# Splitting weights for float32r matmuls: the low parts through accumulating DMAs

## The chip, the cores and the metric

The kernel runs on one core of one Trainium2 chip. The time is what the device takes for one execution, in microseconds (us), from launch to end. A profiled execution has a span of its own, from its first to its last instruction. The core has five engines that run their own instruction streams in order: PE (TensorE, matrix products), DVE (VectorE), ACT (ScalarE), POOL (GpSimd) and SP (SyncE, which here only issues DMAs). They meet through semaphores. Sixteen DMA engines move data between HBM and SBUF, the on-chip memory of 128 partitions.

## The reference

One layer of a streaming encoder, for 512 frames of width 1024, all in float32:

```python
xn = rmsnorm(h, norm_mix_g)
u = xn @ w_in                                   # 7 x 1024 columns
q, k, v, xr, gr, ga, gb = split(u)
ya = chunked_band_attention(q, k, v, rel_table) @ w_attn_out
hr = rg_lru(causal_depthwise_conv(xr, conv_w, conv_b), ...)
yb = (hr * gelu(gr)) @ w_rnn_out
g_a, g_b = sigmoid([ga, gb] + b_merge)
h = h + (g_a * ya + g_b * yb) @ w_o
hn = rmsnorm(h, norm_ffn_g)
g, up = split(hn @ w_ffn_in)                    # 2 x 2816 columns
h = h + (silu(g) * up) @ w_ffn_out
out = rmsnorm(h, final_norm_g)
```

## The kernel before

PE multiplies in float32r, which keeps fewer bits than float32. To get float32 accuracy, each operand is held as two float32r parts: the high part is the rounded number, the low part is what the rounding left. A product `s @ m` is made of three matmuls (`mm3`): high with high (L70), and the two mixed ones (L71, L72). The low part of a weight is read by one of the mixed two: by the third (L72) where the weights are the stationary operand, by the second (L71) where they are the moving one (v, wo, fo).

The weights come in **chunks**, planned in the order of their use: xr, gr, ga, gb (the projections for the recurrent branch and the gates, in pairs of 128-column blocks, j = 0, 2, 4, 6), qk and v (attention), yb, ya, wo, fg and fu (into the feed-forward part), fo (out of it). A plain chunk is one or two times, for wo four times, a tile of 512 KB: 128 partitions by 1024 numbers. The chunks fg2 to fu20 go another way (a Strassen-like scheme, with sums of blocks) and are made by `weight_sums`; the change does not touch them.

For each tile `prefetch` does three things:

- `load` issues a DMA from HBM on SP's queue into a buffer with the tag `raw` (L145). There are three of them, so a load waits until the raw tile three before it has been read for the last time. The Strassen chunks' loads use the same three and one more. Other loads stand in the same SP queue: in attention `bias_tile` (L393) fetches the bias of each head into one of two buffers.
- ACT writes the high part into `hl[:, 0]` of a buffer with the tag `whl` (L76). There are four in `wp`; wo1 and half of the fo chunks have four more of their own. A chunk that feeds 48 matmuls takes two buffers.
- DVE writes the low part, raw minus high, into `hl[:, 1]` (L77). Both lines are in the helper `split`, which also splits activations. Only the second tile of the very first chunk (xr0) has its low part made by POOL (L206).

`weights(name)` makes sure that the named chunk and the one after it have been written down in the program before PE's matmuls on the named one (with other distances in a few places: two for xr, three for fo, none in the first steps). So while PE works on one chunk, ACT and DVE make the next. A `whl` buffer comes free when PE has used it for the last time; the buffers of a chunk are used by its first 128 columns and again by its second.

In order, the stages are: norm and transposes of x; xr, gr, ga, gb with the recurrence between them (40 to 181 us of the span); yb together with the first scores (to 250 us); attention over 16 heads, with the remaining qk, v and ga projections laid between the heads as filling work (to some 420 us); ya; wo; fg0 and fu0; the Strassen chunks (to 756 us); fo and the final norm. In attention POOL also divides the exponentials by their sums (L627), makes one copy of k's low part (L583) and masks the bias (L394); in the recurrence it makes low parts of activations (L457, L500) and one elementwise step (L486).

The order on each engine is laid down when the program is built, from the program order and an estimated timeline; on the chip each engine takes its instructions in that order and waits where it must.

Of the kernel before, what the change touches and what calls it, by code (L numbers as in the profile page):

```python
# [10 lines left out]
AF = mybir.ActivationFunctionType  # L11
ALU = mybir.AluOpType
# [24 lines left out]
def block_kernel(ctx: ExitStack, tc: tile.TileContext, x, norm_mix_g, w_in, b_merge, rel_table,  # L37
# [3 lines left out]
    pe, dve, act, pool, sp = nc.tensor, nc.vector, nc.scalar, nc.gpsimd, nc.sync  # L41
# [20 lines left out]
    def f(ap):  # L62
        return ap.bitcast(F32)
# [10 lines left out]
    def split(hi, lo, src):  # L74

        act.activation(hi, src, AF.Copy)  # L76
        dve.tensor_sub(lo, src, f(hi))  # L77
# [55 lines left out]
    def load(name, k):  # L133
        _, parts, rows, kts = chunks[index[name]]
        wide = sum(width for *_, width in parts)
        n = min(4 * CW // wide, kts - k)
        at = rows + k * P
        pl, bufs = wp, 3
        if name in strassen and name[0] == "f":
            loads[0] += 1  # L140
            pl, bufs = (room[0], 1) if loads[0] % 4 == 0 else (wp, 3)
        raw = pl.tile([P, n, wide], F32, tag="raw", bufs=bufs, name=f"raw_{name}_{k}")
        to = 0
        for src, col, width in parts:
            sp.dma_start(out=raw[:, :, to:to + width],  # L145
                         in_=src[at:at + n * P, col:col + width].rearrange("(k p) e -> p k e", p=P))
            to += width
        raws[name, k] = raw
# [5 lines left out]
    def weight_sums(name):  # L154

        for k in (0, 4):
            if (name, k) not in raws:
                load(name, k)
        r0, r1 = raws.pop((name, 0)), raws.pop((name, 4))
        a11, a21, a12, a22 = r0[:, :, 0:P], r0[:, :, P:CW], r1[:, :, 0:P], r1[:, :, P:CW]  # L160
        sc = room[0]
        s21, s34 = (sc.tile([P, 2, 4, P], F32, tag=tag, bufs=1, name=f"{tag}_{name}")
                    for tag in ("s21", "s34"))
        s2, s1, s3, s4 = s21[:, 0], s21[:, 1], s34[:, 0], s34[:, 1]
        dve.tensor_add(s1, a21, a22)
        dve.tensor_sub(s2, s1, a11)
        other = pool if name in ("fg2", "fu2", "fg4") else dve
        other.tensor_sub(s3, a11, a21)
        other.tensor_sub(s4, a12, s2)
        blocks_ = {}  # L170
        for group in ((("a11", a11), ("a12", a12)), (("s2", s2), ("s1", s1)), (("s3", s3), ("s4", s4)), (("a22", a22),)):
            pl, tag, bufs = sc, "a22", 2
            if len(group) == 2:
                slots[0] += 1
                pl, tag, bufs = (sc, "whl", 1) if slots[0] % 5 == 0 else (wp, "whl", 4)
            o = pl.tile([P, len(group), 2, 4, P], F32R, tag=tag, bufs=bufs, name=f"whl_{name}_{group[0][0]}")
            together = group[0][0] in ("s2", "s3") and name != "fg2"
            if together:
                split(o[:, :, 0], o[:, :, 1], (s21 if group[0][0] == "s2" else s34)[:])
            for i, (key, src) in enumerate(group):  # L180
                if not together:
                    split(o[:, i, 0], o[:, i, 1], src)
                blocks_[key] = o[:, i]
        return blocks_

    def prefetch(n):
        while len(made) < min(n, len(chunks), index.get(barrier[0], len(chunks))):
            name, parts, rows, kts = chunks[len(made)]
            if name in strassen:
                made.append(weight_sums(name))  # L190
                continue
            tiles = []
            wide = sum(width for *_, width in parts)
            step = 4 * CW // wide
            for k in range(0, kts, step):
                n_ = min(step, kts - k)
                if name in extra:
                    hl = extra[name].tile([P, 2, n_, wide], F32R, tag="whl", bufs=4, name=f"whl_{name}_{k}")
                else:
                    hl = wp.tile([P, 2, n_, wide], F32R, tag="whl", bufs=4, name=f"whl_{name}_{k}")  # L200
                if (name, k) not in raws:
                    load(name, k)
                raw = raws.pop((name, k))
                if len(made) == 0 and k:
                    act.activation(hl[:, 0], raw[:], AF.Copy)
                    pool.tensor_sub(hl[:, 1], raw[:], f(hl[:, 0]))  # L206
                else:
                    split(hl[:, 0], hl[:, 1], raw[:])
                tiles.append(hl)
            made.append(lambda part, k, at, tiles=tiles, step=step: tiles[k // step][:, part, k % step, at])  # L210

    def weights(name, ahead=1):
        prefetch(index[name] + 1 + ahead)
        return made[index[name]]
# [70 lines left out]
    for name, w in (("r", w_rg_r), ("i", w_rg_i)):  # L285
        raw = nm.tile([P, 8, P], F32, name=f"wrg_raw_{name}")
# [146 lines left out]
    for name, raw in zip("ri", wrg_raw):  # L433
        hl = rw2.tile([P, 2, 8, P], F32R, bufs=1, name=f"wrg_{name}")
# [305 lines left out]

    hsq = []
    prefetch(index["wo1"] + 1)
    for t in range(NT):
        q2 = cp.tile([P, 2], F32, tag="hsq2", bufs=2, name=f"hsq2_{t}")
# [75 lines left out]
    room[0] = sc  # L820
    barrier[0] = "fo0_16"
    prefetch(index["fg2"] + 1)

    for i, name in enumerate(("fg0", "fg0", "fu0", "fu0")):
# [129 lines left out]
```

## Time and profile before

| | us |
|---|---|
| time, median of 2 runs | 901.03 (900.98 to 901.07) |
| time of the profiled execution | 900.88 |
| its span, first to last instruction | 899.1 |
| mean granted TensorE clock | 0.993 |

The span is 1.8 us shorter than the time of the same execution. Lines of the profile name the engine, the source line (L77 is line 77 of the kernel), the operation, the tile it writes and those it reads (`whl_fo<-raw_fo,whl_fo`; buffer numbers are left out), and partitions x elements. A view that groups instructions gives their count, their durations, the idle time of the engine just before them, and what ended it. A name with a q at its end (SPq) is an engine's queue: the instruction that issues a DMA, not the transfer.

### The profile page before, as it was taken

What the parts mean: (1) busy time and instruction counts of PE and PEld (TensorE: products, weight loads), DVE (VectorE), ACT (ScalarE), POOL (GpSimd) and SP (SyncE); (2) the same over time, 40 slices, a digit from 0 to 9 for tenths busy, and PEclk for the clock granted to TensorE, in tenths of its full rate; (3) what the DMA queues carried; (4) which work ended last, traced back from release to release, by engine and by line L of the source; (5) the groups of instructions that cost most, each with busy time, mean ns of one, the idle gap of its engine ahead of it and who ended that gap; (6) DMA issues with size and microseconds to landing.
All of it is one profiled execution on the core that took longest, in us unless ns stands there. A gap on an engine that the chain in (4) does not pass through costs nothing.

```text
span 899.1 us, 13343 instructions
## 1 busy us (share of the span) xinstructions
PE 881.4 (98%) x5220; PEld 778.1 (87%) x5220; DVE 553.6 (62%) x863; ACT 473.5 (53%) x841; POOL 133.1 (15%) x168
## 2 busy tenths in 40 slices
PE   8999999999999999999999999899999999999997
PEld 5988888888888889797888889899999999888886
DVE  5776556553466676666546455998888887453203
ACT  7566546642257666666533365556555556623103
POOL 4012112120023222222100002510000001300100
PEclk9999999999999999999999999899999999999999
DMA  8323222423332232331123620333433333353002
GB/s 261 95 71 117 85 84 90 118 94 94 105 104 73 74 111 64 93 95 60 66 63 124 217 66 30 117 117 95 140 96 94 96 118 108 98 184 120 30 1 94
DMA packets 85023, 89.05 MB, mean 99 GB/s; under 512 B 5344, under 2 KB 73552, under 8 KB 84960
## 3 DMA queue, kind: packets, MB, share of 16 engines
q1 hardware_dynamic: 83584, 84.73, 30.7%
q10 hardware_dynamic: 1376, 3.47, 1.1%
q8 instruction: 41, 0.67, 0.3%
q14 instruction: 22, 0.18, 0.1%
HBM read 86.05 MB, written 2.14 MB: 98 GB/s over the span
## 4 chain that ended last, share of the span: by engine, by line
PE 92%; DVE 3%; ACT 2%; issue 1%; DMA 1%; POOL 1%; SPq 0%; DVEq 0%; ACTq 0%; POOLq 0%
PE po_out L70 5%; PE po_out L72 5%; PE po_out L71 5%; PE p_fu L71 2%; PE p_fu L70 2%; PE p_fu L72 2%; PE p_fg L72 2%; PE p_fg L71 2%; PE p_fg L70 2%; PE o L659 2%; PE po_ga L70 2%; PE pT L639 2%; PE po_ga L71 2%; PE po_ga L72 2%; PE po_ya L70 2%; PE po_ya L71 2%
## 5 line engine op out<-in xcount | busy, mean ns | idle before, releaser
L70 PE MATMUL po_out<-whl_fo,act_hi 128*128 128x512 f32 (+1 forms) x198 | 73.2, 369 | 0.0
L71 PE MATMUL po_out<-whl_fo,act_hi 128*128 128x512 f32 (+1 forms) x198 | 72.9, 368 | 0.0
L72 PE MATMUL po_out<-whl_fo,act_lo 128*128 128x512 f32 (+1 forms) x198 | 72.1, 368 | 0.0
L77 DVE TENSOR_TENSOR whl_fo<-raw_fo,whl_fo 128x1024 fp32r<-128x1024 f32 x22 | 27.5, 1259 | 47.0 <-ACT whl_fo L76 47.0
L627 POOL TENSOR_SCALAR p<-p,rl 128x128 f32<-128x128 f32 (+1 forms) x64 | 37.4, 605 | 84.4 <-DVE rl L625 83.8
L76 ACT ACTIVATE whl_fo<-raw_fo 128x1024 fp32r<-128x1024 f32 x22 | 23.0, 1056 | 50.6 <-PE po_out L72 36.1
L624 ACT ACTIVATE p<-p,m 128x128 f32<-128x128 f32 (+3 forms) x64 | 35.5, 555 | 22.0 <-DVE m L623 21.6
L623 DVE CUSTOM_DVE_ANT_0 p<-s,bias 128x128 f32<-128x128 f32 (+3 forms) x64 | 29.8, 487 | 22.6 <-PE s L621 21.8
L72 PEld LDWEIGHTS po_out<-whl_fo,act_lo 128*128 128x128 f32 x198 | 37.2, 188 | 6.9
L70 PEld LDWEIGHTS po_out<-whl_fo,act_hi 128*128 128x128 f32 x198 | 37.2, 188 | 6.6
L71 PEld LDWEIGHTS po_out<-whl_fo,act_hi 128*128 128x128 f32 x198 | 37.2, 188 | 6.6
L659 PE MATMUL o<-pp,v 128*128 128x256 f32 (+2 forms) x128 | 35.4, 337 | 3.0 <-ACT pp L76 3.0
L839 POOL TENSOR_TENSOR act_lo<-act,act_hi 128x1024 fp32r<-128x1024 f32 x4 | 10.5, 2624 | 184.1 <-ACT act_hi L838 182.7
L71 PE MATMUL po_v<-whl_v,xnT 128*128 128x256 f32 x128 | 36.9, 288 | 0.0
L77 DVE TENSOR_TENSOR pp<-pT,pp 128x256 fp32r<-128x256 f32 (+2 forms) x64 | 30.4, 486 | 10.4 <-ACT pp L76 10.0
L70 PE MATMUL po_v<-whl_v,xnT 128*128 128x256 f32 x128 | 36.5, 285 | 0.0
L72 PE MATMUL po_v<-whl_v,xnT 128*128 128x256 f32 x128 | 36.4, 284 | 0.0
L76 ACT ACTIVATE pp<-pT 128x256 fp32r<-128x256 f32 (+2 forms) x64 | 26.5, 433 | 10.8 <-DVE pp L77 6.3
L77 DVE TENSOR_TENSOR whl_fu_s<-s_fu,whl_fu_s 128x1024 fp32r<-128x1024 f32 x20 | 25.3, 1280 | 5.7 <-ACT whl_fu_s L76 5.6
L71 PE MATMUL po_xr<-xnT,whl_xr 128*128 128x512 f32 (+1 forms) x80 | 27.9, 354 | 0.6 <-DVE xnT L327 0.5
L639 PE MATMUL pT<-ident,p 128*128 128x128 f32 x160 | 27.5, 273 | 0.7 <-POOL p L627 0.7
L70 PE MATMUL po_gr<-xnT,whl_gr 128*128 128x512 f32 (+1 forms) x80 | 27.8, 349 | 0.1
(354 smaller groups left out, 3089.9 us busy)
## 6 DMA issues: line engine op xcount, KB each, us to landing
raw_fg<-in_w_ffn_in_dram SPq DMA_DIRECT2D x22, 512.0 KB, 4.5
raw_fu<-in_w_ffn_in_dram SPq DMA_DIRECT2D x22, 512.0 KB, 3.6
raw_fo<-in_w_ffn_out_dram SPq DMA_DIRECT2D x22, 512.0 KB, 4.3
raw_qk<-in_w_in_dram SPq DMA_DIRECT2D x32, 256.0 KB, 3.3
raw_xr<-in_w_in_dram SPq DMA_DIRECT2D x8, 512.0 KB, 5.0
raw_gr<-in_w_in_dram SPq DMA_DIRECT2D x8, 512.0 KB, 3.5
raw_ga<-in_w_in_dram SPq DMA_DIRECT2D x8, 512.0 KB, 3.6
raw_gb<-in_w_in_dram SPq DMA_DIRECT2D x8, 512.0 KB, 3.7
```

The costliest lines, as they stand in the source:

```text
L70: pe.matmul(o, sh, mh, start=start, stop=False, skip_group_check=parts)
L71: pe.matmul(o, sh, ml, start=False, stop=False, skip_group_check=parts)
L72: pe.matmul(o, sl, mh, start=False, stop=stop, skip_group_check=parts)
L76: act.activation(hi, src, AF.Copy)
L77: dve.tensor_sub(lo, src, f(hi))
L623: dve.tensor_tensor_reduce(prob[qb][:], sc[:, 0:w], bias[:, S - w:S], -1.0, 3e38, ALU.add, ALU.min, nmax[:, qb:qb + 1])
L624: act.activation(prob[qb][:], prob[qb][:], AF.Exp, bias=nmax[:, qb:qb + 1], scale=-1.0, accum_out=lsum[:, qb:qb + 1])
L627: pool.tensor_scalar(prob[qb][:], prob[qb][:], rl[:, qb:qb + 1], 1.0, ALU.mult, ALU.mult)
L639: pe.transpose(pt[:, at * P:(at + 1) * P], prob[qb][:, kb * P:(kb + 1) * P], ident[:])
L659: pe.matmul(po[:, S - n:S], st, pp[i][:, part, lo:lo + n], start=kb == 0 and part == 0, stop=kb == NT - 1 and part == 1)
L839: (pool if i in (0, 1, 2, 4) else dve).tensor_sub(lo[:], o[:], f(hi[:]))
```

## The change

Every plain chunk but xr0, gr0, fg0 and fu0 gets its low parts in another way. ACT makes the high part as before. POOL writes minus raw into the place of the low part; since that place is float32r, what arrives is minus the rounded number, that is minus the high part. Then POOL issues a DMA that adds raw, read from SBUF, to what stands there. DVE has no part in it any more. The first four plain chunks are split as before, and so are all activations.

```diff
                 if len(made) == 0 and k:
                     act.activation(hl[:, 0], raw[:], AF.Copy)
                     pool.tensor_sub(hl[:, 1], raw[:], f(hl[:, 0]))
+                elif name not in ("xr0", "gr0", "fg0", "fu0"):
+
+                    act.activation(hl[:, 0], raw[:], AF.Copy)
+                    pool.tensor_scalar(hl[:, 1], raw[:], -1.0, None, ALU.mult)
+                    pool.dma_start(out=hl[:, 1], in_=raw[:], accum_op=ALU.add)
                 else:
                     split(hl[:, 0], hl[:, 1], raw[:])
                 tiles.append(hl)
```

## The prediction, made before the changed kernel had run

> **What bounds the kernel.** I read the busy times first, then stretches of the span, then what PE waited for. The first line gives each engine's busy time, its share of the span and its instructions.
>
> ```profile
> PE 881.4 (98%) x5220; PEld 778.1 (87%) x5220; DVE 553.6 (62%) x863; ACT 473.5 (53%) x841; POOL 133.1 (15%) x168
> ```
>
> PE is busy for all but 17.7 us of the span of 899.1. The next view cuts the span by stage; its columns after the stretch are its length, busy time (instructions) of PE, weight loads, DVE, ACT and POOL, the granted clock, the DMA share and GB/s.
>
> ```profile
> core 0: us, PE busy (x) PEld busy (x) DVE busy (x) ACT busy (x) POOL busy (x), PEclk, DMA share, GB/s
> ...
> 40.00:181.00 141.00, 141.00 (x621) 116.23 (x620) 92.72 (x121) 85.97 (x112) 26.52 (x24) 1.00 0.32 97
> ...
> 250.00:420.00 170.00, 165.09 (x972) 145.32 (x971) 110.42 (x249) 110.03 (x249) 46.11 (x91) 0.99 0.30 89
> 420.00:494.00 74.00, 74.00 (x348) 60.96 (x347) 40.84 (x69) 32.27 (x57) 4.74 (x10) 1.00 0.23 74
> ...
> 756.00:828.00 72.00, 72.00 (x371) 61.07 (x370) 34.23 (x32) 31.74 (x38) 8.10 (x3) 1.00 0.39 125
> ```
>
> In the stages with plain chunks PE has no gap at all, but for 4.9 us in attention (170.00 - 165.09). So DVE's 92.72 of 141 us in the first stretch are hidden, and taking work from DVE cannot shorten it. What PE waited for, all in all:
>
> ```profile
> PE o L659 <- ACT pp L76: 3.0, 2, 1.5
> PE q_fg L70 <- ACT whl_fg_s L76: 1.9, 1, 1.9
> ...
> PE pT L639 <- POOL p L627: 0.7, 2, 0.3
> ...
> PE po_gr L72 <- DVE whl_gr L77: 0.3, 1, 0.3
> ```
>
> A low part of a plain weight made PE wait once, for 0.3 us, and that one is gr0's, which the change leaves alone. The 3.0 us for the transposed probabilities are a chain ACT to DVE in attention that a freer DVE may shorten. Hence a gain has a ceiling of about 5 us (the 4.9 of attention), and the question is how much of the cover the slower way to a low part uses up.
>
> **Removed: DVE's subtractions.**
>
> ```profile
> L77 DVE TENSOR_TENSOR whl_fo<-raw_fo,whl_fo x22: 1218/1225/2002, 756.2 to 854.5; 128x1024 fp32r<-128x1024 f32 x22
> ...
> L77 DVE TENSOR_TENSOR whl_qk<-raw_qk,whl_qk x16: 1211/1226/1422, 167.4 to 383.2; 128x1024 fp32r<-128x1024 f32 x16
> ...
> L77 DVE TENSOR_TENSOR whl_gr<-raw_gr,whl_gr x8: 1209/1225/2284, 15.5 to 151.3; 128x1024 fp32r<-128x1024 f32 x8
> ...
> L77 DVE TENSOR_TENSOR whl_xr<-raw_xr,whl_xr x7: 1216/1226/1254, 8.6 to 135.1; 128x1024 fp32r<-128x1024 f32 x7
> ```
>
> 22 for fo, 16 for qk, six each for gr and xr (two and one are of the excluded chunks), and eight each for ga, gb, v, yb, ya and wo by the plan of chunks: 98 tiles. At 1.225 us they are 120 us of DVE. By the windows PE gains from this only in attention; I take 2 us of the 3.0.
>
> **Added: 98 negations and 98 accumulating DMAs.** A negation is one operation on 128x1024. The nearest rows are POOL's own elementwise ones:
>
> ```profile
> L486 POOL TENSOR_SCALAR a<-u 128x512 f32<-128x512 f32 x8 | 4.9, 618 | 33.8 <-DVE u L484 33.7
> ...
> L839 POOL TENSOR_TENSOR act_lo<-act,act_hi 128x1024 fp32r<-128x1024 f32 x4 | 10.5, 2624 | 184.1 <-ACT act_hi L838 182.7 <-DMA g_fin<-in_final_norm_g_dram 1.4
> ```
>
> Below is 0.62 (the same kind on half the elements), above 2.62 (the same size with two inputs); I take twice 0.618, 1.2 us, the same kind. No POOL-issued DMA and no accumulating one stand in this trace. What stands there are SP's loads:
>
> ```profile
> q1 hardware_dynamic: 83584, 84.73, 30.7%
> q10 hardware_dynamic: 1376, 3.47, 1.1%
> ```
> ```profile
> L145 SPq DMA_DIRECT2D raw_wo<-in_w_o_dram x8: 367/368/368, 470.0 to 497.3; - x8
> ...
> DMA to landing us min/median/max: 3.5/3.6/8.0
> ```
>
> Issue: 0.37 us (SP's row) at least, 2.62 (POOL's long row above) at most, if the issue occupies POOL like a long instruction of its own; I take 1.0, between the two and nearer to the row of an issue. Transfer: q1 used 0.307 x 16 x 899.1 = 4416 engine-us for 84.73 MB, so a tile of 0.524 MB takes 27.3, or 1.7 us of all 16 engines; q10, by the same sum, 1.5 us. The add reads two tiles and writes one: one pass, 1.5, is the floor; two passes at q10's price, 3.0, is my value; two at q1's with one load ahead, 2 x 1.7 + 1.7 = 5.1, is the top. A load's landing of 3.5 less its 1.7 leaves 1.8 of latency. So the add lands 4.8 us after its issue (3.3 to 6.9).
>
> The Trainium skill, "Collectives: The Full Stack", section "The bandwidth ceiling: the fold count and why AG ≠ RS ≠ AR", says that the add inside a DMA costs nothing in itself, but its second source halves the rate. No run here shows it yet; by it the transfer would be the same two passes.
>
> From a free buffer with its raw tile there, the low part then takes 1.2 + 1.0 + 4.8 = **7.0 us** (4.3 to 12.1). Before it took ACT's 1.06 and DVE's 1.23, 2.3 us. It is 4.7 us later (2.0 to 9.8). Set against the typical time until PE wants it, here for ga2:
>
> ```profile
> L72 PE MATMUL po_ga<-xnT,whl_ga x16: 389/389/398, 88.8 to 99.0; 128*128 128x512 f32 x16
> L76 ACT ACTIVATE whl_ga<-raw_ga x2: 1061/1062/1062, 72.1 to 74.8; 128x1024 fp32r<-128x1024 f32 x2
> ...
>   PE po_xr L72: 2.6, 2
> ```
>
> ACT starts on each tile when PE's po_xr frees the buffer, at 72.1 and 74.8, and the first L72 on it comes at 88.8, so there are 16.7 us: 7.0 fits, and 12.1 too. PE takes 10.2 us over 15 steps of three matmuls, 10.9 for a chunk; the DMA engines would have two loads and two adds in it, 3.4 + 6.0 = 9.4 us. Full, but not over.
>
> **The tight places.** ga0, at the start:
>
> ```profile
> L72 PE MATMUL po_ga<-xnT,whl_ga x16: 389/389/398, 39.5 to 51.2; 128*128 128x512 f32 x16
> L76 ACT ACTIVATE whl_ga<-raw_ga x2: 1045/1052/1059, 30.2 to 35.3; 128x1024 fp32r<-128x1024 f32 x2
> ```
>
> The first tile has 9.3 us. The second is first read four steps (2.7 us) later, at 42.2, so it has 6.9 against 7.0: with some queueing 0.5 us. For wo:
>
> ```profile
> L76 ACT ACTIVATE whl_wo<-raw_wo x8: 1046/1062/1062, 480.8 to 505.5; 128x1024 fp32r<-128x1024 f32 x8
> L77 DVE TENSOR_TENSOR whl_wo<-raw_wo,whl_wo x8: 1218/1224/1226, 481.9 to 506.6; 128x1024 fp32r<-128x1024 f32 x8
> ```
> ```profile
> L752 DVE SCALAR_TENSOR_TENSOR h<-po_h,h x8: 683/692/692, 503.2 to 540.2; 128x512 f32<-128x512 f32 x8
> ...
> L727 ACTq DMA_DIRECT2D h<-in_x_dram x4: 357/443/459, 494.8 to 496.2; - x4
> ```
>
> Eight tiles pass through three raw buffers. The last load went out at 497.3, when tile 5 had been split, and its low part was done at 507.8 (506.6 + 1.22), in the middle of the eight products that ended between 503.2 and 540.2. Tile 5's add lands 4.7 us later, and so do the last load and its own add: the load came beside the four h loads and took the longest, 8.0 us; later it would come after them and take 3.6, which makes good the first delay, but the add at the end costs 4.7 again. So the last low part is some 4.7 late. If PE's order is as before it waits 4 us; if its order moves the other products of the first half forward, 0; if each reuse adds its delay, 9. I take 4. At fo's start:
>
> ```profile
> L71 PE MATMUL po_out<-whl_fo,act_hi x22: 388/393/399, 766.3 to 784.4; 128*128 128x512 f32 x22
> ...
> L76 ACT ACTIVATE whl_fo<-raw_fo x7: 1038/1050/1062, 755.1 to 780.4; 128x1024 fp32r<-128x1024 f32 x7
> ```
>
> 11.2 us: nothing at 7.0, 1 us at 12.1.
>
> **What is queued behind.** On POOL 98 x 2.2 = 216 us come in (133 becomes 349, 39%). In the window of attention its 46 us get some 24 x 2.2 = 53 more, and the division of the probabilities (L627), for which pT waited 0.7 us, stands in that queue; I set this against what DVE's relief gives beyond the 2 us. On SP a load waits for its raw buffer, now until the add has landed, and what is behind it waits too, above all the bias of a head:
>
> ```profile
> 283.92 0.37 SPq L145 DMA_DIRECT2D raw_v<-in_w_in_dram  x1
> 285.26 7.06 SPq L393 DMA_DIRECT2D bias<-ext_d  x2
> ...
> 333.65 0.37 SPq L145 DMA_DIRECT2D raw_v<-in_w_in_dram  x1
> 334.30 8.08 SPq L393 DMA_DIRECT2D bias<-ext_d  x2
> ```
>
> Here a bias follows within 1.3 and 0.7 us on a load that a low part had released; I count four such heads. Each gets its bias up to 4.7 us later, 19 us in all; the filling matmuls between the heads cover most. I take 4.
>
> Sum: 0.5 + 4 + 4 - 2 = +6.5 us on the profiled execution's 900.9, so 907; the median of the runs, 901.03, is the same within 0.2.
>
> **The rivals.**
> - *The cover holds and attention gains.* PE's order follows the later low parts, nothing stalls, and the 4.9 us come in: 896. For it speaks the 16.7 us; against it that wo's eighth tile came 507.8, late already. 0.10.
> - *SP's queue.* The four heads are not covered, and the delay of 4.7 each goes through to the transposes: 19 instead of 4, 922. It decides from about 4.5 us of lateness per head, since 18 us are the 2%. For it speaks that pT has waited for POOL's p at all, against it PE's mere 4.9 us of gaps in attention. 0.10.
> - *DVE holds POOL up.* The slowest DVE subtractions took 2284 and 2002 ns beside a median of 1225: something excluded them for about 1 us. If each negation and each issue waits out one DVE instruction of 1.2 us, the low part takes 9.4, with a second one behind it 12: ga0 then loses 3 to 5 us, wo 9, fo 1, attention 7: +20, 921. The Trainium skill, "SBUF — State Buffer", section "Who interferes with whom", has such a lock between a DVE instruction with two SBUF inputs and a POOL instruction that reads SBUF, and adds that a DVE in a two-port mode keeps POOL from writing descriptors; by that rule the trace's long subtractions agree, and no run yet shows the descriptors. 0.08.
> - *The DMA engines become the bound.* From (10.9 - 3.4) / 2 = 3.75 us per add on they cannot keep up with PE. At the top, 5.1, a chunk takes 13.6 us, 2.7 more; over 20 dense chunks (12 of xr to gb, 4 of yb, 4 of ya) that is 54 us, 955. Against it: 5.1 needs three tiles' worth of traffic per add. 0.15.
>
> The add might also not give the low part at all, if POOL's rounding differs from ACT's; that would not change the time.
>
> **The numbers.** My forecast has 0.56, between 899 and 918. A measurement of this kernel tells 2%, 18 us, from no change. Faster by more than that has no mechanism, as PE's gaps are 17.7 us in all: 0.01. Slower by more: 0.10 + 0.08 + 0.15 = 0.33. Within: 0.66. The range goes from the gain's 896 up to 938, short of the middle of the last rival, and leaves out some 0.14.
>
> **What would show it.** In the changed profile: no L77 for whl tiles but the excluded and Strassen ones, DVE near 434 us; POOL near 350; a DMA queue of its own with some 51 MB; PE waiting for a DMA that writes whl_wo and whl_ga, not whl_gr or whl_gb; adds landing near 5 us after their issue. If PE waits for whl in every dense chunk, the DMA rival is right; if pT or s waits with bias loads late on SP, the queue; if POOL's negations are far over 1.2 us, the lock. I am wrong on the main point if an add takes more than 9 us from issue to landing, or if DVE's relief shows where PE had no gap.

## The result, and the profile after

The changed kernel takes 991.88 us (median of 2 runs, 990.47 and 993.30) beside 901.03: the ratio is 1.101, with a 95% interval from 1.094 to 1.108. It is 10% slower, where 907 was forecast and 938 was the end of the range. The profiled execution is the one of 990.47 us, with a span of 988.7.

From the page of the changed kernel, the busy time of each engine and two of the DMA queues (packets, MB, share of 16 engines):

```profile
PE 906.8 (92%) x5220; PEld 788.9 (80%) x5220; DVE 445.2 (45%) x765; ACT 473.7 (48%) x841; POOL 479.4 (48%) x364
...
q0 software_dynamic: 14112, 51.39, 29.3%
q1 hardware_dynamic: 83584, 84.73, 27.0%
```

The change did what it says: DVE has 98 instructions less, POOL 196 more, and a new queue moves 51.39 MB. But PE is now idle for 81.9 us (988.7 - 906.8) instead of 17.7, and the same 5220 matmuls keep it busy for 25.4 us more. The 89.6 us that the span grew are these two: 64.2 of gaps and 25.4 of slower matmuls. POOL is at 479 us instead of the 349 that I had summed up.

What PE waited for in the changed kernel (total us, times, longest):

```profile
PE po_out L71 <- DMA whl_fo<-raw_fo: 18.9, 7, 7.0
PE po_h L71 <- DMA whl_wo<-raw_wo: 11.2, 3, 8.3
PE s L625 <- ACT kh L587: 8.4, 2, 5.8
PE q_fg L70 <- ACT whl_fg_s L76: 5.9, 1, 5.9
PE s L625 <- DVE m L628: 5.4, 4, 1.8
```

The low parts of fo and wo, now written by a DMA, come late; and in attention PE waits for ACT and DVE, which have no more to do than before. The lines behind the new work on POOL, from the groups of instructions of the changed kernel, and from the view of the tile whl_fo from 826 us on (durations min/median/max in ns; the last line is the adds' time from issue to landing):

```profile
L210 POOL TENSOR_SCALAR whl_fo<-raw_fo 128x1024 fp32r<-128x1024 f32 x22 | 61.0, 2783 | 52.4 <-DMA raw_fo<-in_w_ffn_out_dram 46.4 <-PE q_fg L72 5.1 <-PE q_fu L72 1.0
...
L211 POOL DMA_DIRECT2D whl_qk<-raw_qk x16 | 14.3, 928 | 0.6 <-issue 0.6
```
```profile
L210 POOL TENSOR_SCALAR whl_fo<-raw_fo x20: 2761/2767/3096, 824.0 to 956.3; 128x1024 fp32r<-128x1024 f32 x20
...
DMA to landing us min/median/max: 4.5/6.7/11.1
```

A negation takes 2.77 us, not 1.2; the issue of an add 0.93, and the add lands after 4.5 us at best. POOL's order in fo, from the timeline of POOL (start, duration, then what and how often; in brackets the idle time before and what ended it):

```profile
864.26 8.25 POOL L210 TENSOR_SCALAR whl_fo<-raw_fo 128x1024 fp32r<-128x1024 f32 x3 [9.78 <-DMA raw_fo<-in_w_ffn_out_dram]
872.46 2.68 POOL L211 DMA_DIRECT2D whl_fo<-raw_fo  x3
885.02 8.25 POOL L210 TENSOR_SCALAR whl_fo<-raw_fo 128x1024 fp32r<-128x1024 f32 x3 [9.88 <-DMA raw_fo<-in_w_ffn_out_dram]
```

POOL negates three tiles, then issues three adds, then waits for the next three raw tiles, which can only be loaded into the buffers that these adds have read. One round is 8.25 + 2.68 + 9.88, or 20.8 us from 864.26 to 885.02. PE's matmuls on three tiles take 16.4 (5.45 us per tile, half of the 10.9 per chunk of the prediction), so each round leaves a gap of some 4.4 us. SP's queue shows the same loop; in the waits of SP before and after, the fo loads are held up by

```profile
SPq L145 <- DVE whl_fo L77: 70.8, 19, 14.8
```
```profile
SPq L145 <- DMA whl_fo<-raw_fo: 128.5, 19, 16.4
```

Where the time went, by stages that I cut at the first matmul on po_h (wo) and on po_out (fo); the last five rows are experiments told below:

| us | start to wo | wo, f0, Strassen | fo | span |
|---|---|---|---|---|
| before | 494.6 | 271.4 | 133.0 | 899.1 |
| after | 522.6 | 304.0 | 162.1 | 988.7 |
| short negation (e1_two_op) | 498.7 | 284.1 | 133.5 | 916.3 |
| long negation, in turn (e5_in_turn) | 537.4 | 283.9 | 136.9 | 958.2 |
| after's order, short (e12) | 498.4 | 301.3 | 134.7 | 934.4 |
| e1's order, long (e13) | 514.8 | 289.0 | 141.4 | 945.2 |
| POOL subtracts, no add (e3) | 498.8 | 273.7 | 133.1 | 905.6 |

Each of the three parts lost about 30 us (28.0, 32.6 and 29.1). But the first cut does not part the same work everywhere. In the changed kernel PE does a single matmul on po_h at 522.6, goes back to 44 matmuls of ya, and takes up wo at 533.2; from the views of the tiles po_ya and whl_wo (count, durations, then first and last start):

```profile
L72 PE MATMUL po_ya<-aT,whl_ya x64: 390/397/400, 485.4 to 533.0; 128*128 128x512 f32 x64
...
L71 PE MATMUL po_h<-whl_wo,mT x64: 387/389/794, 533.2 to 591.8; 128*128 128x512 f32 x64
```

Of the other rows only e12 has the same 44, some 10 us of PE without a gap. Counted to the last matmul of ya instead, the changed kernel lost 39 us up to wo, 22 from there to fo, and 29 in fo.

### The profile page after: what moved, and what is told of

Same layout as the page of the kernel before. It is cut to its first block, busy times and chain, and to the rows that moved or that the text cites. A ratio compares the mean times of both kernels' runs of the same rounds, so it can differ in the third digit from the quotient of the medians.

```text
span 988.7 us, 13608 instructions
## 1 busy us (share of the span) xinstructions
PE 906.8 (92%) x5220; PEld 788.9 (80%) x5220; DVE 445.2 (45%) x765; ACT 473.7 (48%) x841; POOL 479.4 (48%) x364
## 3 DMA queue, kind: packets, MB, share of 16 engines
q0 software_dynamic: 14112, 51.39, 29.3%
## 4 chain that ended last, share of the span: by engine, by line
PE 48%; DMA 27%; POOL 11%; ACT 5%; issue 4%; DVE 4%; SPq 0%; POOLq 0%; ACTq 0%; DVEq 0%
DMA whl_fo<-raw_fo 5%; POOL whl_fo L210 3%; DMA raw_fo<-in_w_ffn_out_dram 3%; DMA raw_wo<-in_w_o_dram 2%; PE p_fg L72 2%; PE p_fg L70 2%; PE p_fg L71 2%; DMA raw_v<-in_w_in_dram 2%; PE p_fu L70 2%; PE p_fu L71 2%; PE p_fu L72 2%; DMA whl_gr<-raw_gr 2%; DMA raw_qk<-in_w_in_dram 2%; DMA whl_wo<-raw_wo 2%; PE o L664 2%
## 5 line engine op out<-in xcount | busy, mean ns | idle before, releaser
L210 POOL TENSOR_SCALAR whl_fo<-raw_fo 128x1024 fp32r<-128x1024 f32 x22 | 61.0, 2783 | 52.4 <-DMA raw_fo<-in_w_ffn_out_dram 46.4
L72 PE MATMUL po_out<-whl_fo,act_lo 128*128 128x512 f32 (+1 forms) x198 | 74.5, 383 | 0.0
L210 POOL TENSOR_SCALAR whl_qk<-raw_qk 128x1024 fp32r<-128x1024 f32 x16 | 44.9, 2810 | 36.5 <-DMA raw_qk<-in_w_in_dram 18.8
L71 PEld LDWEIGHTS po_out<-whl_fo,act_hi 128*128 128x128 f32 x198 | 39.1, 198 | 28.4 <-DMA whl_fo<-raw_fo 21.3
L882 DVE TENSOR_TENSOR h<-po_out,h 128x512 f32<-128x512 f32 (+1 forms) x9 | 5.7, 629 | 110.6 <-PE po_out L72 110.6
L77 DVE TENSOR_TENSOR pp<-pT,pp 128x512 fp32r<-128x512 f32 (+1 forms) x64 | 30.6, 488 | 43.2 <-ACT pp L76 42.8
L70 PEld LDWEIGHTS po_out<-whl_fo,act_hi 128*128 128x128 f32 x198 | 38.5, 195 | 7.2
L76 ACT ACTIVATE pp<-pT 128x512 fp32r<-128x512 f32 (+1 forms) x64 | 26.6, 432 | 32.1 <-PE pT L644 28.2
L70 PE MATMUL po_v<-whl_v,xnT 128*128 128x256 f32 x128 | 37.6, 295 | 3.0 <-ACT whl_v L209 2.6
L71 PE MATMUL po_v<-whl_v,xnT 128*128 128x256 f32 x128 | 38.1, 298 | 2.1 <-DMA whl_v<-raw_v 2.1
L72 PE MATMUL po_v<-whl_v,xnT 128*128 128x256 f32 x128 | 37.5, 293 | 0.0
L210 POOL TENSOR_SCALAR whl_wo<-raw_wo 128x1024 fp32r<-128x1024 f32 x8 | 22.4, 2805 | 31.0 <-DMA raw_wo<-in_w_o_dram 30.9
L71 PE MATMUL po_h<-whl_wo,mT 128*128 128x512 f32 x64 | 25.9, 410 | 11.2 <-DMA whl_wo<-raw_wo 11.2
```

Of the source, the lines that this page charges most:

```text
L70: pe.matmul(o, sh, mh, start=start, stop=False, skip_group_check=parts)
L71: pe.matmul(o, sh, ml, start=False, stop=False, skip_group_check=parts)
L72: pe.matmul(o, sl, mh, start=False, stop=stop, skip_group_check=parts)
L210: pool.tensor_scalar(hl[:, 1], raw[:], -1.0, None, ALU.mult)
```

## The experiments

Each time stands beside runs of the kernel before on the same chip (902.03 for e1 to e4, 900.82 for e5 to e7, 901.55 from e8 on). Where no interval is given it is one execution. Three theories stood at the start. A: the loop through the three raw buffers is too long. B: POOL's queue. C: the DMA engines are too full.

**e1_two_op: the negation in another form.** The row of 618 ns that I had doubled is of an instruction with two operations (L486 multiplies and adds); the change's has one. So the same negation, written with two:

```diff
-                    pool.tensor_scalar(hl[:, 1], raw[:], -1.0, None, ALU.mult)
+                    pool.tensor_scalar(hl[:, 1], raw[:], -1.0, 1.0, ALU.mult, ALU.mult)
```

> The negation is written with two immediates (times -1, times 1), the form of the row that took 618 ns on 512 elements, instead of one operation; the value is the same. Changed kernel: 990.5 us, negation 2.77 us. Theory A (the loop through the three raw buffers, load + negation + issue + add, is as long as PE takes for three tiles, so PE stalls wherever there is no stock): the negation falls to about 1.2 us, the loop from some 16 to 14.4 us, and the stalls of wo, fo and attention shrink: about 955. Theory B (POOL's queue: 3.7 us a tile among its other work): POOL falls from 479 to about 325 us busy, about 925. Theory C (the 16 DMA engines are too full, share 0.75, and loads and adds slow each other): traffic is the same, no less than 980. If the form makes no difference to the negation's 2.77 us, the run tells nothing of the three.

Measured: 918.07. Groups of POOL's instructions in it, and what PE waited for:

```profile
L210 POOL TENSOR_SCALAR whl_qk<-raw_qk 128x1024 fp32r<-128x1024 f32 x16 | 17.9, 1122 | 33.2 <-issue 12.8 <-PE po_k L72 9.7 <-PE po_yb L72 6.1
L211 POOL DMA_DIRECT2D whl_qk<-raw_qk x16 | 14.2, 906 | 4.5 <-POOL whl_qk L210 4.5
```
```profile
PE po_h L71 <- DMA whl_wo<-raw_wo: 5.6, 1, 5.6
PE q_fg L70 <- ACT whl_fg_s L76: 5.0, 1, 5.0
```

The negation takes 1.12 us, and 74 of the 91 us are gone, with the same adds and the same traffic. That refutes C, and it is more than A or B had given it (955 and 925). What is left is at wo, as forecast, and just behind it.

**e2_act_neg: the negation on ACT.**

```diff
-                    pool.tensor_scalar(hl[:, 1], raw[:], -1.0, None, ALU.mult)
+                    act.activation(hl[:, 1], raw[:], AF.Copy, scale=-1.0)
```

> ACT writes minus raw (Copy with scale -1) in place of POOL; POOL only issues the adds. ACT gets 98 x 1.06 = 104 us (474 to 578), POOL loses 98 x 2.8 = 274 (479 to about 205). Theory A: the loop is 1.7 us shorter, and an issue no longer stands behind the next negation: about 950. Theory B: nearly all of the loss on POOL's account goes: about 915. Theory C: no less than 980.

Measured: 922.53. POOL, with the issues alone, is down to 207 us, ACT up to 562. PE waits 5.4 us at wo and in a few places for ACT. It comes out near e1: the negation has to be short, and on which of the two engines it runs made 4 us.

**e3_pool_sub: POOL subtracts, no DMA.**

```diff
-                    pool.tensor_scalar(hl[:, 1], raw[:], -1.0, None, ALU.mult)
-                    pool.dma_start(out=hl[:, 1], in_=raw[:], accum_op=ALU.add)
+                    pool.tensor_sub(hl[:, 1], raw[:], f(hl[:, 0]))
```

> POOL makes the low part in one subtraction (raw minus high) and there is no add by DMA. The low part is then ready 1.06 + about 2.6 = 3.7 us after the buffer is free. Theory A: 905, since the loop is 3.5 + 3.7 = 7 us and raw comes free at POOL's end. Theory B: POOL is still busy for some 390 us in the same places, so much of the loss stays: about 940. Theory C: the adds' traffic is gone, so 905 as well; this run separates B from A and C.

Measured: 907.37. A subtraction takes POOL 2.4 to 2.7 us, about as long as the slow negation, and costs only 5 us in all. So an instruction of 2.7 us per tile on POOL is not enough, and B falls as it stood; it takes the add behind it.

**e4_raw_fo: more raw buffers for half of fo.** Half of the fo chunks get three raw buffers of their own.

```diff
+        if name in extra and name != "wo1":
+            pl, bufs = extra[name], 3
         raw = pl.tile([P, n, wide], F32, tag="raw", bufs=bufs, name=f"raw_{name}_{k}")
```

> Half of the fo chunks (those that have whl buffers of their own) get three raw buffers of their own, so fo's loads have six instead of three; all else as in the changed kernel. Theory A: fo, 162 us long against 133 before, loses most of its 29 us: about 965, and its PE waits for whl_fo go from 18.9 to under 5 us. Theory B: the loads come sooner but POOL is as busy: 985. Theory C: no change in fo, 990.

Measured: 981.02, a gain of some 10 us, all in fo (162 to 152), and less than A expected. POOL's timeline in it shows why:

```profile
847.86 14.30 POOL L212 TENSOR_SCALAR whl_fo<-raw_fo 128x1024 fp32r<-128x1024 f32 x5 [5.02 <-DMA raw_fo<-in_w_ffn_out_dram]
862.11 1.76 POOL L213 DMA_DIRECT2D whl_fo<-raw_fo  x2
```

With six buffers the order has five negations in a row, 14.3 us, ahead of the first add, and PE waited 12.4 us for a low part once. So the order of POOL's queue may be what costs: the adds stand behind the negations of tiles that are needed later.

**e5_in_turn: negation, add, negation, add.** The long negation stays, each queued behind the add of the tile before.

```diff
+                    with tc.issue_after(lastadd[0]) if lastadd[0] is not None else ExitStack():
-                    pool.tensor_scalar(hl[:, 1], raw[:], -1.0, None, ALU.mult)
-                    pool.dma_start(out=hl[:, 1], in_=raw[:], accum_op=ALU.add)
+                        pool.tensor_scalar(hl[:, 1], raw[:], -1.0, None, ALU.mult)
+                    lastadd[0] = pool.dma_start(out=hl[:, 1], in_=raw[:], accum_op=ALU.add).ins
```

> Edit: the slow one-operation negation (2.77 us) stays, but each negation is queued on POOL behind the add of the tile before, so that POOL's order is negation, add, negation, add. Nothing is left out. Theory D (the length of the negation is what costs): POOL's time per tile is 2.77 + 0.9 either way, the waits for whl_fo and whl_wo stay, and it takes 975 to 995. Theory E (the order costs: the changed kernel lets three negations go ahead of three adds, so that the first add is issued 5.5 us late and all three land behind each other at 4.7, 6.7 and 10 us): in turn a raw buffer is held for 3.6 + 2.8 + 0.9 + 4.7 = 12 us, or 4.0 per tile with three buffers, under PE's 5.45; fo falls from 162 to about 134, attention from 283 to about 255, and only wo still waits, some 4 to 8 us more than with the short negation (918): 920 to 932.

Measured: 959.98, between D and E. fo fell to 136.9, as E expects, and the part from wo to the Strassen stage got 20 us shorter, of which 10 are the matmuls of ya that are back in front of the cut. Attention, from the first matmul on po_yb to the first on po_ya, stayed at 278.8 us (283.3 in the changed kernel, 251.0 before), which E does not explain, and the start of wo came 15 us later, 10 of them those matmuls.

**e6_short_wo_dve: short negation, wo left to DVE.**

```diff
-                elif name not in ("xr0", "gr0", "fg0", "fu0"):
+                elif name not in ("xr0", "gr0", "fg0", "fu0") and name[:2] != "wo":
```

> Edit: the negation in the form with two operations (1.05 to 1.27 us), and wo's eight tiles keep DVE's subtraction; nothing is left out. With the short negation everywhere the time was 918.1 beside 902.0, with 53.2 us in wo (45.4 before), 26.2 in f0 (24.6) and 204.7 in the Strassen stage (201.4). Theory F (the 7.8 of wo come from its last tiles' adds, and f0 and the Strassen stage are late because the raw buffers of wo come free late): without wo's adds all three return, and it takes 903 to 907, though 90 adds with their 47 MB still run. Theory C (the traffic of the adds itself slows the loads or PE): 910 or more.

Measured: 905.78, ratio 1.0057 (1.0036 to 1.0078). F holds: wo is back at 45.4, f0 at 24.6, the Strassen stage at 200.9. Ninety adds, with short negations, cost 5 us in all; wo's eight had cost some 11 (918.07 - 902.03, less 5).

**e7_attention_only: the gain that I had hoped for.** The add, with the short negation, only for 20 tiles of attention:

```diff
-                elif name not in ("xr0", "gr0", "fg0", "fu0"):
+                elif name[:2] == "qk" and name != "qk0" or name[0] == "v" and name != "v0":
```

> Edit: the add only for the chunks of attention after the first (qk1 to qk7, v1 to v3), 20 tiles, with the negation of two operations; all the rest is as before; nothing is left out. Theory G (as I forecast: a DVE with 24 us less to do in attention lets PE gain there, up to the 4.9 us of its gaps): 897 to 901 beside 901 to 902. Theory H (DVE does not set attention's pace: with all of the short adds attention took 252.4 beside 251.0, so there is nothing to gain): 901 to 904.

Measured: 901.12 beside 900.82, ratio 1.0005 (0.9994 to 1.0016). H: no gain from a freer DVE, in the place with the best chance of one. Attention itself took 249.5 us instead of 251.0 in the one execution profiled, which the times do not show.

**e8_pool_high and e9_in_turn_pool_high: who stands in ACT's queue.** In attention, the timeline of the changed kernel shows PE's longest gap like this:

```profile
274.95 0.90 POOL L211 DMA_DIRECT2D whl_qk<-raw_qk  x1
...
279.61 0.37 SPq L145 DMA_DIRECT2D raw_v<-in_w_in_dram  x1
...
285.29 1.06 ACT L209 ACTIVATE whl_v<-raw_v 128x1024 fp32r<-128x1024 f32 x1 [4.86 <-DMA raw_v<-in_w_in_dram]
...
286.37 0.59 ACT L665 ACTIVATE oacc<-o 64x512 f32<-64x512 f32 x1
286.99 0.59 ACT L587 ACTIVATE kh<-po_k 64x512 fp32r<-64x512 f32 x1
...
287.63 1.12 PE L625 MATMUL s<-kh,q 128*128 128x256 f32 x3 [5.77 <-ACT kh L587]
```

The tile of v is loaded late, because its buffer was held until the add that was issued at 274.95 had landed: SP waited 9.7 us for that `DMA whl_qk<-raw_qk` before it issued the load at 279.61, and the load took 5.7 us to land. ACT, in order, waits for it with the high part, behind which stands the key part that PE needs. Such waits for raw tiles in attention are not in the trace of before. The edit lets POOL make the high parts of attention's 40 tiles, in e9 on top of e5_in_turn:

```diff
-                    act.activation(hl[:, 0], raw[:], AF.Copy)
+                    if name in ("ga4", "ga6") or name[:2] in ("qk", "yb") and name != "qk0" or name[0] == "v" and name != "v0":
+                        pool.tensor_copy(hl[:, 0], raw[:])
+                    else:
+                        act.activation(hl[:, 0], raw[:], AF.Copy)
```

> Edit: the changed kernel, but for the 40 tiles that are split during attention (qk1 to qk7, v1 to v3, yb, ga4, ga6) the high part is copied by POOL, right before the negation, and not by ACT. Nothing is left out. In the changed kernel ACT's high part waited at the head of ACT's queue for a raw tile that was loaded late (whl_v for 4.86 us at 285.29, with oacc, kh and pp behind it, and PE 5.77 us for that kh). Theory I (this wait in ACT's queue is what stretches attention): without it attention falls from 283 us to 262 or less, and the whole to 970 or less, though POOL gets 40 x 1.2 to 2.5 us more. Theory J (POOL's own queue stretches attention, by negations and adds among the probabilities and key parts): POOL has still more to do, attention stays at 280 or more, the whole at 988 or more.

> Edit: as e5_in_turn (long negation, each behind the add of the tile before), and the high part of attention's 40 tiles by POOL. Nothing is left out. e5_in_turn took 959.98 us, with 278.8 in attention and a 9.0 us wait of PE for kh. Theory I (ACT's queue): attention 262 or less, 940 to 945 in all. Theory J (POOL's queue): attention 279 or more, 960 or more.

Measured: 993.94 and 981.29. PE's longest wait for kh fell from 5.8 to 2.3 us and from 9.0 to 2.0, but the sum of these waits did not (8.4 and 8.6 us, 9.0 and 10.8), and attention got longer (291.1 and 300.7). In e8, with copies of 1.04 to 1.10 us more on POOL, PE's waits for the adds of v and yb rose from 2.1 to 9.9 us in that stretch. I falls as the sole cause; J's numbers are met.

**e10_in_turn_short: in turn, with the short negation.** The edits of e1 and e5 together.

> Edit: the short negation of two operations, and each negation queued behind the add of the tile before. Nothing is left out. With the short negation alone the time was 918.1, and most adds were issued 0.4 us after their negation by themselves. Theory E (the order only matters by the time that an add spends behind other negations): 915 to 921, and wo still near 53 us. Theory K (putting the negations in turn costs by itself, as a negation that waits for its raw tile now stands ahead of other POOL work; in e5_in_turn the stage of xr to gb took 146.1 us with 12.9 of gaps, against 2.7 of gaps without it): 925 or more, with gaps in the stage of xr to gb.

Measured: 916.70, with 51.8 us in wo, so E. With a short negation most adds stand right behind theirs anyway.

**e11_pool_two_ops: POOL as busy, without the add.** This tests J by itself.

```diff
-                    pool.tensor_scalar(hl[:, 1], raw[:], -1.0, None, ALU.mult)
-                    pool.dma_start(out=hl[:, 1], in_=raw[:], accum_op=ALU.add)
+                    pool.tensor_sub(hl[:, 1], raw[:], f(hl[:, 0]))
+                    pool.tensor_scalar(hl[:, 1], f(hl[:, 1]), 1.0, 1.0, ALU.mult, ALU.mult)
```

> Edit: no negation and no add; POOL subtracts the high part from the raw tile as in e3_pool_sub (2.4 to 2.7 us) and then multiplies the low part by one in place with the short form (1.1 us). Nothing is left out. POOL is so occupied for some 3.6 us per tile, as by the long negation and the issue of the add in the changed kernel (2.77 + 0.9), but the raw tile is free after the subtraction, and no transfer stands between. Theory J (POOL's occupation alone stretches attention from 254 us, at 2.5 us per tile, to 280): attention 275 or more, 930 or more in all. Theory L (it takes both: the raw tile held through the negation, the queue and the 4.6 us of the add, so that loads, then the high parts at the head of ACT's queue, then the probabilities come late, and the long negation in the same queue): attention 262 or less, 908 to 920 in all.

Measured: 912.35. The stretches of attention in the changed kernel and in this one (length, then busy time of PE, weight loads, DVE, ACT, POOL, the granted clock, DMA share, GB/s):

```profile
201.70:485.00 283.30, 260.46 (x1414) 223.62 (x1414) 108.13 (x282) 143.96 (x312) 179.29 (x182) 0.96 0.64 145
```
```profile
205.00:455.00 250.00, 245.21 (x1368) 211.78 (x1367) 109.04 (x277) 138.81 (x305) 166.38 (x177) 1.00 0.30 87
```

POOL does about the same work in both (166 and 179 us), and without the adds attention takes 250. The first stretch holds 46 matmuls more: in that order they are of v's first projection and come later, some 5.5 us at 0.12 each. The gaps of PE differ by 18 us (22.8 and 4.8). J falls, and L's numbers are met: POOL's occupation alone costs nothing there, and it takes the add as well. That it is the raw tile, held until the add has landed, is argued from the wait above.

**e12_order_kept_short and e13_short_order_long: length or order.** The order on each engine is laid down anew for each kernel, so e1 had changed two things. Here the order is kept, and only afterwards the form of the negations is exchanged (e12; in e13 the other way, on e1's program):

```diff
+    for fn in nc.m.functions:
+        for b in fn.blocks:
+            b.instructions = [other_form(i) if i.name in negations else i for i in b.instructions]
     r = _run(nc, [arrays], core_ids=[0])
```

> Edit: the program of the changed kernel with its order on every engine as it was laid down; only then each of the 98 negations is replaced by the form with two operations (1.1 us instead of 2.77). Nothing is left out. e1_two_op has the same form, but its order was laid down anew, so that it changed two things. Theory D (the length on the chip costs): fo's three negations and three adds now take 20.8 - 3 x 1.65 = 15.9 us for three tiles, under PE's 16.4, so fo falls from 162 to about 136, attention from 283 to about 256, and the whole to 915 to 930. Theory M (the order laid down for the long form costs, with its negations ahead of adds): fo stays over 150 and attention over 270: 955 or more.

> Edit: the program of e1_two_op (918.07) with its order kept; only then each negation is replaced by the form with one operation (2.77 us). Nothing is left out. Theory D (length): each tile's low part comes 1.65 us later and each engine's queue behind it too; attention over 270, wo over 58, 955 to 990. Theory M (order): an add stands right behind its negation, a raw tile is held 1.65 us longer, and only wo loses some 5 us more: 920 to 930.

Measured: 936.14 and 946.95. Neither theory has it alone. With the runs of e1 and of the changed kernel:

| time, us | short negation | long negation |
|---|---|---|
| order laid down for the short | 918.1 | 947.0 |
| order laid down for the long | 936.1 | 991.9 |

The length alone costs 29, the order alone 18, both together 74: 27 us come only where they meet. The table of stages shows where. Counted to the last matmul of ya (498.5 us in e1, 508.7 in e12, 514.6 in e13, 533.0 in the changed kernel), up to wo the order costs 10 us and the length 16, and both together 34. From wo to the Strassen stage the order costs 7 and the length 5. In fo either alone is nearly covered (1.2 and 7.9), and together they cost 28.6, so that most of what neither explains alone is in fo. POOL's timeline in e12 shows both. In fo:

```profile
831.84 1.04 POOL L210 TENSOR_SCALAR whl_fo<-raw_fo 128x1024 fp32r<-128x1024 f32 x1 [9.73 <-DMA raw_fo<-in_w_ffn_out_dram]
...
835.59 2.66 POOL L211 DMA_DIRECT2D whl_fo<-raw_fo  x3
848.38 1.04 POOL L210 TENSOR_SCALAR whl_fo<-raw_fo 128x1024 fp32r<-128x1024 f32 x1 [10.14 <-DMA raw_fo<-in_w_ffn_out_dram]
```

The same three and three, but a round is 16.5 us (848.38 - 831.84) instead of 20.8, and that is PE's 16.4. And at wo:

```profile
520.87 1.03 POOL L210 TENSOR_SCALAR whl_wo<-raw_wo 128x1024 fp32r<-128x1024 f32 x1 [8.81 <-DMA raw_wo<-in_w_o_dram]
525.70 1.04 POOL L210 TENSOR_SCALAR whl_wo<-raw_wo 128x1024 fp32r<-128x1024 f32 x1 [3.79 <-DMA raw_wo<-in_w_o_dram]
528.22 1.04 POOL L210 TENSOR_SCALAR whl_wo<-raw_wo 128x1024 fp32r<-128x1024 f32 x1 [1.47 <-DMA raw_wo<-in_w_o_dram]
529.20 2.67 POOL L211 DMA_DIRECT2D whl_wo<-raw_wo  x3
541.69 1.04 POOL L210 TENSOR_SCALAR whl_wo<-raw_wo 128x1024 fp32r<-128x1024 f32 x1 [9.82 <-DMA raw_wo<-in_w_o_dram]
```

The first of these tiles is negated at 521.9, but its add waits 7.3 us more behind two negations whose raw tiles come late. Its raw buffer takes the last load, and so the last low part of wo is negated only at 541.7.

## Why the prediction was wrong, step by step

**The step that failed: the price of the negation.** I took "twice 0.618, 1.2 us, the same kind". The name and the shape of that row were the same, but not the operations: L486 multiplies and adds, the change's instruction only multiplies. With two operations the estimate was right (1.12 us in e1); with one it took 2.77, over the upper bound of 2.62. In the order that was laid down for the long form this term alone is worth 56 us (e12, 936.1), and with an order to suit it 74 (e1). The code had shown the difference. Priced right, it would have moved my sum by a few us only, as my top of 12.1 us a tile had 2.62 for it: what made so much of 1.6 us a tile are the next two steps.

**The step that was missing: the queue between negation and add.** "From a free buffer with its raw tile there" I added 1.2 + 1.0 + 4.8, as if each add left right after its negation. In the order laid down for the long form it stands behind one to three other negations. I had named POOL's queue only for the probabilities. The order as a whole is worth 45 us: the same long negations in e1's order take 947.0 (e13).

**The cover was set against the wrong time.** I set 7.0 and 12.1 us against 16.7 us from a free whl buffer to PE's first use, which is a budget of one tile. What decides is the loop of the three raw buffers: 20.8 us for three tiles in fo against PE's 16.4. I counted that loop at wo only. With the negation at 2.77 and everything in turn (e5) fo nearly fits again; with the short one it fits in either order (e1, e12).

**Right: the add itself.** The issue was put at 1.0 us and took 0.93 in the group of qk, at most 1.19 in the other groups. The transfer was put at 3.0 us of all 16 engines: 29.3% of 16 x 988.7 for 98 adds is 47.3 engine-us each, 2.96 us. The rule of the Trainium skill that I had weighed there ("Collectives: The Full Stack", section "The bandwidth ceiling: the fold count and why AG ≠ RS ≠ AR"; a second source halves the rate) fits: a load took 1.65 us by the same sum, and the add 1.8 times that. Landing at 4.8 is what an add alone needs (4.5 at least); the median for fo is 6.7, where three are issued in a row. The longest took 11.1 in fo and 12.8 in wo, over the 9 that I had named as a sign of being wrong on the main point.

**Right in kind, small in size: wo.** I forecast a wait of 4 us there; e1 has 5.6, and by e6 wo's adds cost 11 with what stands behind them: beside before, e1 takes 7.8 us more in wo, 1.6 in f0 (fg0 and fu0) and 3.3 in the Strassen stage, and in e6 all three are back. I had reckoned with the wait alone.

**Wrong, and small: the gain of 2 us in attention.** e7 shows none.

**The rivals.** The cover that holds (896) had the wrong sign, as nothing gains (e7). The DMA engines as the bound (955) are refuted by e1 and e12: the same adds, 918 and 936. SP's queue with its bias loads did not show as such: among the waits of DVE, which reads the bias, none is for it, and the 4 us that I had put into the sum have no counterpart. What did stand in a queue behind a late raw tile was ACT's key part. DVE holding POOL up did not happen either: the negations took 2761 at least and 2767 in the median, so nearly none had to wait. Its sign, negations far over 1.2 us, came true through the form of the instruction. And none of my rivals was the one that came about, a slower stage in a ring of buffers, although each term of it stood in the text.

**What stays open.** Of the three things that the changed kernel has in attention, the long negation, the add and the order, e3, e11 and e1 each leave out at least one and stay between 250 and 254 us. But e12, with the short negation in the long form's order, takes 268.3, and so does e13 (268.2), with the long one in e1's order; PE's gaps in them are 13.0 and 17.5 us, beside 5.8 in e1 and 22.8 in the changed kernel. Why this order costs even a short negation 7 us more of gaps there is open. Which of the chains through ACT, DVE, POOL and SP carries how much of the 39 us lost up to wo was not separated; e8 and e9 only show that taking these high parts from ACT does not help.

## What to carry to other kernels

Price a new instruction by a row with the same operations and operands, and look at the code of that row: name and shape are not enough, and the difference here was 2.77 to 1.12 us. When a producer gets slower, add up how long one buffer is held over all its stations, divide by the number of buffers, and set that against what the consumer takes per tile; the slack of a single tile says nothing about it. And an asynchronous step that is issued from an engine's queue begins when that queue gets to it: ask which instructions the order puts ahead.

## What the hardware showed that I had not expected

*Two operations are quicker than one.* On POOL a multiplication of 128x1024 float32 into float32r took 2.77 us with one operation and 1.04 to 1.28 with two (means of the groups in e1, e10 and e12). ACT took 1.04 for the same. Why, no run here shows.

*Short gaps can cost more than themselves.* Most of the 25.4 us of slower matmuls are the granted clock: PE was busy for 43 us at half the clock in the changed kernel and for 9 before, and half of the difference, 17 us, is what this clock costs by that sum. The other 8 are not accounted for. Three stretches of the changed kernel around a gap of 8 us at wo, and four of the kernel before around two gaps of 1.5 us (columns as above; the clock is the third number from the end):

```profile
540.00:548.00 8.00, 0.00 (x0) 0.00 (x0) 0.00 (x0) 0.00 (x0) 0.00 (x0) 0.50 1.04 265
548.00:551.80 3.80, 3.40 (x7) 2.29 (x8) 0.00 (x0) 0.61 (x1) 0.61 (x1) 0.50 0.89 245
551.80:560.00 8.20, 8.20 (x37) 6.77 (x37) 1.38 (x2) 3.07 (x5) 8.20 (x5) 1.00 0.20 66
```
```profile
363.00:365.10 2.10, 0.57 (x5) 0.40 (x3) 1.69 (x2) 2.08 (x6) 0.60 (x1) 1.00 1.01 265
365.10:370.00 4.90, 4.73 (x21) 3.84 (x22) 1.51 (x4) 1.63 (x3) 2.81 (x6) 1.00 0.49 151
...
413.70:416.20 2.50, 0.82 (x5) 0.59 (x5) 1.71 (x4) 2.45 (x6) 2.05 (x3) 1.00 0.86 292
416.20:419.60 3.40, 3.40 (x10) 2.73 (x10) 1.32 (x3) 1.03 (x3) 2.33 (x5) 0.50 0.49 161
```

After the gap of 8 us PE runs at half the clock for a while, and the gap at 413.7 was enough for 3.4 us of it. The one at 363.5, as long, was followed by none, and neither was one of 2.6 us at 188.8 in the changed kernel. What decides between them is not shown. The Trainium skill, "TensorE: Matmul & The Clock Gate", section "Part 1: The HAM clock gate (the "warmup" mystery)", has the same two states and the same 3.4 us to come back, but the fall to half only after an idle window of about 3.4 us; here 1.5 us did it at 413.7.

*Subtractions on POOL slow DVE down.* DVE's total with POOL's negations on ACT (e2) and with POOL's subtractions (e3), the same 765 DVE instructions:

```profile
PE 886.9 (96%) x5220; PEld 780.2 (85%) x5220; DVE 433.5 (47%) x765; ACT 562.0 (61%) x939; POOL 207.1 (22%) x266
```
```profile
PE 883.2 (98%) x5220; PEld 778.7 (86%) x5220; DVE 491.6 (54%) x765; ACT 471.6 (52%) x841; POOL 364.2 (40%) x266
```

They are 58 us longer beside the subtractions, and 12 longer beside the changed kernel's negations (445.2). Which of them grew is seen in two rows, first in e2, then in e3 (busy us, mean ns); the first of each pair reads two tiles in SBUF, the second one in SBUF and one in PSUM, where PE's products are written:

```profile
L720 DVE TENSOR_TENSOR za<-za,zb 128x512 f32<-128x512 f32 x8 | 5.4, 689 | 0.1
L719 DVE SCALAR_TENSOR_TENSOR za<-za,po_ya 128x512 f32<-128x512 f32 x8 | 5.4, 685 | 13.9 <-PE po_ya L72 13.9
```
```profile
L719 DVE TENSOR_TENSOR za<-za,zb 128x512 f32<-128x512 f32 x8 | 14.9, 1868 | 0.1
L718 DVE SCALAR_TENSOR_TENSOR za<-za,po_ya 128x512 f32<-128x512 f32 x8 | 5.3, 679 | 5.5 <-PE po_ya L72 5.5
```

The one took 1868 ns instead of 689, the other 679 instead of 685. The Trainium skill, "SBUF — State Buffer", section "Who interferes with whom", has a DVE instruction with two SBUF inputs contend with a POOL instruction that reads SBUF; the traces agree by these rows, and show that the subtractions did it far more than the negations.
